# SwiGLU input projections of a decoder trunk: standing weights and 256 moving columns, from the third channel block on

## The chip, the cores and the metric

The kernel runs on one core of one Trainium2 chip. The metric is device time in microseconds (us), median of three runs; lower is better. The engines are named as in the profile: PE is TensorE, PEld its weight loads, DVE is VectorE, ACT is ScalarE, POOL is GpSimd, SP issues most DMAs. Of a matrix product one operand stands in the PE array (it is loaded by a weight load, LDWEIGHTS), the other one moves through it (MATMUL).

## The reference, cut to what matters

The trunk has 256 tokens of 1024 channels, two layers, and in each layer a SwiGLU, a token mixer and a second SwiGLU. There are thus four SwiGLU stages (f00, f01, f10, f11), and the change lies in them alone:

```
D_MODEL = 1024; SEQ = 256; D_FF = 2816

def swiglu(x, w_in, w_out):
    gate, up = jnp.split(x @ w_in, 2, axis=-1)
    return (jax.nn.silu(gate) * up) @ w_out

x = layer_norm(DN_ALPHA * x + 0.5 * swiglu(x, ffn_w_in[i, 0], ffn_w_out[i, 0]), ln_g[i, 0], ln_b[i, 0])
```

Everything is float32.

## The kernel before, in words

Products in float32 are made of three one-pass products of rounded values (type float32r). Each operand is split exactly into a rounded part and the rest: ACT casts (L113 for weights, L207 for activations), DVE subtracts (L114, L208). `mm3` (L199) then multiplies rounded by rounded (L201), rounded by weight rest (L202) and activation rest by rounded weight (L203), all into one accumulator in PSUM.

The 256 tokens are two blocks m of 128, the 2816 hidden channels are 11 blocks c of 256 (NB = 11). For a channel block c the input projection takes 256 gate columns and the 256 up columns that belong to them: 512 columns, in four weight units of 2 x 128 rows by 512 columns (`def_cols`). Before, the activations stand: `proj` loads 128 input channels by 128 tokens as weights (`lhsT=xs`) and moves 512 weight columns, so the PSUM bank holds 128 tokens by 512 columns (256 of gate, 256 of up). For a block c that is 2 token blocks x 8 groups of input channels x 3 = 48 products of 512 columns. `done` (L361 to L367) evacuates each bank: ACT takes Silu of the gate half (L365), DVE multiplies it by the up half (L366). The result `h` is tokens first, and the output projection needs it channels first, so `T(c)` (L369 to L380) turns it with four PE transposes of 128x128 (L376) into a PSUM bank `tp`, from where `split` (L206 to L208) makes `hT`. The output projection `O(c, m)` (L382) has `hT` standing and 512 columns of `ffn_w_out` moving: 12 products for each token block, into four accumulators (`acc`) that stay open over the whole stage.

The order on PE and SP is that of the list of operations: PE and SP are scheduled by hand, one operation after the other as `op` recorded them. In a stage the blocks c = 0 and 1 go first, one token block at a time (`proj_seq`, with T(0)); then for c = 2 to 10 the loop does the input projection of c for both token blocks (`proj_both`: four quarters), `T(c - 1)`, and the output products `O(c - 2, 0)` and `O(c - 2, 1)`. The stage ends with `O(8, 0)`, `T(10)`, `O(9, 0)`, `O(10, 0)`, the layer norm of token block 0, and `O(8..10, 1)`. Weight units come by DMA into four staging places and are split into a ring of ten (`Stream.advance`, called ahead of every operation). `mmp` has two PSUM banks for `mm`, `tp` two, `accp` four. `to_cm` (L218) makes the channels-first activations `xh` and `xl`, one pair of tiles for each token block.

Of the kernel before, what the change touches and what calls it, by code (L numbers as in the profile page):

```python
# [22 lines left out]
P = 128  # L23
# [29 lines left out]


class Stream:
    """Weight units in the order of their use: each is loaded ahead of time and split
    exactly into a rounded part and the rest, which one-pass products carry."""

    def __init__(self, tc, raw, wh, wl):
        self.tc, self.nc, self.raw, self.wh, self.wl = tc, tc.nc, raw, wh, wl  # L60
# [7 lines left out]
        return len(self.units) - 1  # L68

    def free(self, now, v):  # L70
        """The next place of the ring for unit v, if the work issued up to op `now` is done with it."""
        shut = min((i for i in self.shut if i > now), default=1 << 30)
        n = N_W + (N_WX if self.ext and self.last[v] < shut else 0)
        for d in range(n):
            t = (self.turn + d) % n
            u = self.ring[t]
            if u is None or self.last[u] <= now:
                return t
        return None

    def load(self, now, upto=None):
        """Load what the staging places allow after the work issued up to op `now`."""
        while len(self.loaded) < (upto or len(self.units)):
            v = len(self.loaded)
            o = v - N_RAW
            if o >= 0 and (len(self.done) <= o or o in self.native and self.last[o] > now):
                break
            t = self.raw.tile([P, 1024], F32, tag="raw", name=f"raw{v}")
            for view, src in self.units[v]:
                self.nc.sync.dma_start(view(t), src)  # L90
            self.loaded.append(t)

    def advance(self, now, ahead, upto=None):
        """Split the units that have a place, some ahead of use; `upto` must have one."""
        nc = self.nc
        self.top = max(self.top, -1 if upto is None else upto)
        n = len(self.units)
        self.load(now)
        while len(self.done) < min(n, self.top + 1 + ahead, len(self.loaded)):
            u = len(self.done)  # L100
            raw = self.loaded[u]
            if u in self.native:
                self.done.append((raw, None))
                continue
            t = self.free(now, u)
            if t is None:
                break
            hp, lp = (self.ext, self.ext) if t >= N_W else (self.wh, self.wl)
            self.ring[t] = u
            self.turn = t + 1  # L110
            h = hp.tile([P, 1024], F32R, tag=f"wh{t}", name=f"wh{u}", bufs=1)
            l = lp.tile([P, 1024], F32R, tag=f"wl{t}", name=f"wl{u}", bufs=1)
            nc.scalar.copy(h, raw)  # L113
            nc.vector.tensor_tensor(l, raw, h.bitcast(F32), op=ALU.subtract)  # L114
            self.loaded[u] = None
            self.done.append((h, l))
            self.load(now)
        assert upto is None or upto < len(self.done), "no place for a weight unit"
# [2 lines left out]
        return self.done[i]  # L121


class Builder:
    def __init__(self, tc, aps, pools):
        self.tc, self.nc, self.a = tc, tc.nc, aps
# [10 lines left out]
        self.first = {}  # L137

    def extra(self, kind):
        """The room next to the lasting pools: more weight units, or more 4 KB tiles."""  # L140
        if self.ext:
            self.ext.close()
        self.ext = contextlib.ExitStack()
        pool = self.ext.enter_context(self.tc.tile_pool(name="ext" + kind, bufs=1, reuse_waits="tile"))
        self.ws.ext = pool if kind == "w" else None
        self.xpool = pool if kind == "s" else None

# [1 line left out]
    def op(self, fn, *keys):  # L149
        self.ops.append((fn, keys, self.ahead))  # L150

    def flush(self):
        """The last normalisation of the stage before, behind the first work of this one."""
        if self.late:
            self.op(self.late)
        self.late = None
# [59 lines left out]
            evac(q, ps)  # L216

    def to_cm(self, src):  # L218
        """[tokens, channels] -> rounded part and rest, [channel, block of channels, token]."""
        h, l = self.s4("xh", F32R), self.s4("xl", F32R)  # L220

        def evac(q, ps):
            s = slice(q * 512, q * 512 + 512)
            self.split(h[:, s], l[:, s], ps)

        self.transpose8(src, evac)
        return h, l
# [42 lines left out]
        return xn  # L270

    def proj(self, ps, m, xs, key, us):
        """ps[128 tokens, 512] += x[m] @ units us of key (two blocks of 128 rows each)."""
        for u in us:
            h, l = self.w((key, u))
            for k in range(2):
                kk = 2 * u + k
                s = slice(k * 512, k * 512 + 512)
                c = slice(kk * P, kk * P + P)
                if l is None:  # L280
                    i = self.nc.tensor.matmul(ps, lhsT=xs[:, c], rhs=h[:, s], start=kk == 0, stop=kk == 7)  # L281
                else:
                    i = self.mm3(ps, xs[0][:, c], xs[1][:, c], h[:, s], l[:, s], kk == 0, kk == 7)
                self.first.setdefault(key, i)

    def def_cols(self, key, src, cols):
        """Units of src[1024, columns]: 2 blocks of 128 rows by 512 columns each."""
        v = src.rearrange("(k p) f -> p k f", p=P)
        w = 512 // len(cols)
        for u in range(4):  # L290
            parts = []
            for i, c in enumerate(cols):
                parts.append((
                    lambda t, i=i, w=w: t.rearrange("p (k g f) -> p k g f", k=2, f=w)[:, :, i, :],
                    v[:, 2 * u:2 * u + 2, c:c + w]))
            self.defs[key, u] = parts
# [5 lines left out]
        self.defs[key] = [(lambda t: t, src)]  # L302

    def proj_both(self, key, xs, done, between=None):
        """Both token blocks, two units at a time; between[i]: ops before the i-th quarter."""
        st = {}

        def go(m, us):
            def f():
                if m not in st:  # L310
                    st[m] = self.mmb()
                self.proj(st[m], m, xs()[m], key, us)
                if us[-1] == 3:
                    done(m, st[m])
            return f

        for i, (us, m) in enumerate((([0, 1], 0), ([0, 1], 1), ([2, 3], 0), ([2, 3], 1))):
            for fn in (between or {}).get(i, ()):
                self.op(fn)
            self.op(go(m, us), *[(key, u) for u in us])  # L320
# [15 lines left out]
                self.op(fn)  # L336
            self.op(go([2 * i, 2 * i + 1]), (key, 2 * i), (key, 2 * i + 1))

# [1 line left out]
    def ffn(self, i, j, S, hooks=(), store=None):  # L340
        nc = self.nc
        win, wout = self.a["ffn_w_in"][i, j], self.a["ffn_w_out"][i, j]
# [7 lines left out]

        def cm(m):
            def f():
                st["xs"][m] = self.to_cm(S["x"][m])
            return f

        def start():
# [12 lines left out]
        def T(c):  # L369
            def f():  # L370
# [7 lines left out]
                self.split(t[:, 0:512], t[:, 512:1024], ps)  # L378
                st["hT"][c] = t
            return f  # L380

        def O(c, m, ns=(0, 1)):  # L382
            def f():
# [31 lines left out]
        for c in range(2, NB):  # L415
# [3 lines left out]
                self.op(hooks[c == NB - 3])  # L419
            if c >= NB - 2:  # L420
                self.ahead = 99
            self.proj_both((tag, "i", c), xs, done(c))
            self.op(T(c - 1))
            if c >= 2 and c < NB - 1:
                O(c - 2, 0)
                O(c - 2, 1)
        L = NB - 1
        O(L - 2, 0)
        self.op(T(L))
        O(L - 1, 0)  # L430
        O(L, 0)
        self.ahead = AHEAD
# [3 lines left out]
                O(c, 1, ns)  # L436
        self.late = ln(1)

# [1 line left out]
    def sgu(self, S):  # L440
        nc = self.nc
        a = self.a
# [176 lines left out]
            O(3, i, 1)  # L619
        self.late = ln(1)  # L620

# [1 line left out]
    def rwkv(self, S):  # L623
        """The loads and the preparation that may come before the stage, and the stage."""
        nc = self.nc
        a = {k[5:]: v for k, v in self.a.items() if k.startswith("rwkv_")}
        V, G, A = nc.vector, nc.gpsimd, nc.scalar
# [101 lines left out]
            return f  # L729

        def lora1(m):
            """The first products of both small nets, with a row of ones below for the second's bias."""
            def f():
                ps = self.tpb()
                for i, x in enumerate((st["xf"][m], st["xx"][m])):
# [30 lines left out]
            return f  # L766

        def decay_x(m):
            """What stood before each token: the row above, or 1 at the start of a chunk."""
            def f():  # L770
                Ep, Em, Ex = st["E"][m]
                for c in range(2):
# [3 lines left out]
            return f  # L776

        def decay_w(m):
            """A chunk's last row is the decay of the whole chunk."""
            def f():  # L780
                if m == 0:
                    st["wc"] = self.small("wc", [P, 4, 8])
# [126 lines left out]
            return f  # L909

        def cm_kb(m, i, q):
            """Chunk 0 has its keys before its b's, chunk 1 behind."""
            def f():
                if i == 1 and q == 0:
                    st["KBT", m] = [self.s4("KBT") for q in range(2)]
# [141 lines left out]
        col = lambda h: slice((h // 2) * 64, (h // 2) * 64 + 64)  # L1057

        class Chunk:
            """One chunk of 64 tokens; v's in the half of the partitions that is the chunk's, u's in the other."""  # L1060

            def __init__(c_, ch):
                c_.ch, c_.m, c_.c = ch, ch // 2, ch % 2
# [8 lines left out]
            def at(c_, h, z, rows):  # L1072
                o = (h // 2) * P + z * 64
                return st["A"][c_.ch][h % 2][rows, o:o + 64]
# [294 lines left out]
```

## Time and profile before

| | |
|---|---|
| device time, three runs | 1148.21, 1146.11, 1149.02 us; median 1148.21 |
| span of the profiled execution | 1146.8 us |
| median less span | 1.4 us |
| PE busy | 1103.2 us, 96% of the span, 5854 products |
| DVE, ACT, POOL busy | 698.1, 481.2, 42.3 us |
| DMA | 216.51 MB, mean 189 GB/s |

The profiled execution's own time is known by its span alone; it lies within the three runs. Busy shares are means over the span: PE was at 100% in the SwiGLU stages, less in the RWKV stage and at the start. The length of a PE row is the time from a product's start to its modelled end, and the rows overlap; what a product costs in a stream is the distance from its start to the start of the next one.

### The profile page before, as it was taken

The numbers are of one execution on the slowest core, as the hardware profiler recorded it, in microseconds if no ns is written. First come the engines' busy times: TensorE is split into PE (matmuls) and PEld (weight loads), VectorE is DVE, ScalarE is ACT, GpSimd is POOL, SyncE is SP. The second block draws the span as 40 slices with busy tenths as digits, with TensorE's granted clock in tenths as the row PEclk, the third lists the DMA queues.
The fourth block names the chain that finished last, engine by engine and source line by source line (L and its number), as shares of the span: only waits on it lengthen the run. The fifth ranks groups of instructions, "written<-read, shape, count | busy, mean of one in ns | idle before, by whom it ended". The sixth has DMA issues, their size and how long they took to land.

```text
span 1146.8 us, 15330 instructions
## 1 busy us (share of the span) xinstructions
PE 1103.2 (96%) x5854; PEld 878.3 (77%) x5854; DVE 698.1 (61%) x964; ACT 481.2 (42%) x632; POOL 42.3 (4%) x44
## 2 busy tenths in 40 slices
PE   7999999999999999999999999999989889999997
PEld 5788888778888888888788888775555768888885
DVE  5654556769658555457655453878655788555544
ACT  5544444455335444444444452462123145444430
POOL 0000000100000000000000000112100110000000
PEclk9999999999999999999999999999998999999999
DMA  8776565776644766655567563437876135766631
GB/s 277 244 236 187 182 196 168 233 254 201 215 147 151 243 204 199 187 184 154 189 218 224 184 199 125 165 93 251 269 203 222 60 123 190 245 201 196 184 111 37
DMA packets 153788, 216.51 MB, mean 189 GB/s; under 512 B 21197, under 2 KB 114829, under 8 KB 153714
## 3 DMA queue, kind: packets, MB, share of 16 engines
q1 hardware_dynamic: 152250, 210.80, 57.5%
q0 software_dynamic: 1024, 3.15, 1.0%
q10 hardware_dynamic: 440, 1.57, 0.5%
q8 instruction: 46, 0.75, 0.3%
q14 instruction: 28, 0.23, 0.1%
HBM read 209.46 MB, written 3.42 MB: 186 GB/s over the span
## 4 chain that ended last, share of the span: by engine, by line
PE 77%; DVE 8%; DMA 7%; issue 3%; ACT 2%; SPq 1%; POOL 1%; ACTq 0%; DVEq 0%; POOLq 0%
PE mm L201 14%; PE mm L203 14%; PE mm L202 14%; PE acc L201 8%; PE acc L203 8%; PE acc L202 8%; PE mm L281 3%; DMA raw<-ffn_w_in 3%; DVE wl L114 2%; PE tp L376 2%; ACT wh L113 1%; DMA raw<-sgu_w_in 1%; POOL rs L239 1%; SPq L90 1%; PE tp L215 1%
## 5 line engine op out<-in xcount | busy, mean ns | idle before, releaser
L114 DVE TENSOR_TENSOR wl<-raw,wh 128x1024 fp32r<-128x1024 f32 x328 | 396.2, 1221 | 272.7 <-ACT wh L113 264.7
L113 ACT CAST wh<-raw 128x1024 fp32r<-128x1024 f32 x328 | 340.4, 1051 | 347.7 <-PE acc L203 144.1
L201 PE MATMUL mm<-wh,xh 128*128 128x512 f32 x832 | 327.6, 394 | 8.3 <-DVE h L366 3.8
L202 PE MATMUL mm<-wl,xh 128*128 128x512 f32 x832 | 325.1, 391 | 1.2 <-DVE wl L114 1.2
L203 PE MATMUL mm<-wh,xl 128*128 128x512 f32 x832 | 325.1, 391 | 0.2 <-DVE xl L208 0.2
L201 PEld LDWEIGHTS mm<-wh,xh 128*128 128x128 f32 x832 | 156.6, 188 | 44.9 <-DVE h L366 5.5
L202 PEld LDWEIGHTS mm<-wl,xh 128*128 128x128 f32 x832 | 156.6, 188 | 34.8 <-DVE wl L114 3.2
L203 PEld LDWEIGHTS mm<-wh,xl 128*128 128x128 f32 x832 | 156.5, 188 | 34.4 <-DVE xl L208 1.9
L201 PE MATMUL acc<-wh,hT 128*128 128x512 f32 x352 | 140.9, 400 | 0.0
L203 PE MATMUL acc<-wh,hT 128*128 128x512 f32 x352 | 137.6, 391 | 0.0
L202 PE MATMUL acc<-wl,hT 128*128 128x512 f32 x352 | 137.2, 390 | 0.0
L365 ACT ACTIVATE h<-mm 128x256 f32<-128x256 f32 x88 | 33.8, 384 | 104.1 <-PE mm L203 104.1
L203 PEld LDWEIGHTS acc<-wh,hT 128*128 128x128 f32 x352 | 66.1, 188 | 14.3
L202 PEld LDWEIGHTS acc<-wl,hT 128*128 128x128 f32 x352 | 66.3, 188 | 12.8
L201 PEld LDWEIGHTS acc<-wh,hT 128*128 128x128 f32 x352 | 66.1, 188 | 12.5
L366 DVE TENSOR_TENSOR h<-h,mm 128x256 f32<-128x256 f32 x88 | 36.7, 417 | 58.8 <-ACT h L365 58.8
L281 PE MATMUL mm<-raw,mix 128*128 128x512 f32 x128 | 60.6, 619 | 0.7 <-DMA raw<-rwkv_w_rkv 0.7
L239 POOL TENSOR_TENSOR rs<-ve,mhalf 128x1 f32<-128x1 f32 x14 | 14.1, 1010 | 928.0 <-DVE ve L247 928.0
L281 PEld LDWEIGHTS mm<-raw,mix 128*128 128x128 f32 x128 | 24.0, 196 | 27.2 <-issue 25.1
L208 DVE TENSOR_TENSOR hT<-tp,hT 128x512 fp32r<-128x512 f32 x44 | 30.1, 684 | 7.6 <-ACT hT L207 7.6
L207 ACT CAST hT<-tp 128x512 fp32r<-128x512 f32 x44 | 25.8, 587 | 9.0 <-PE tp L376 8.9
L261 DVE SCALAR_TENSOR_TENSOR y<-acc,x 128x512 f32<-128x512 f32 x24 | 15.9, 685 | 18.7 <-PE acc L203 18.7
(189 smaller groups left out, 878.4 us busy)
## 6 DMA issues: line engine op xcount, KB each, us to landing
raw<-ffn_w_in SPq DMA_DIRECT2D x352, 256.0 KB, 3.9
raw<-ffn_w_out SPq DMA_DIRECT2D x88, 512.0 KB, 3.9
raw<-rwkv_w_rkv SPq DMA_DIRECT2D x40, 512.0 KB, 4.0
raw<-sgu_w_in SPq DMA_DIRECT2D x32, 512.0 KB, 4.9
raw<-sgu_w_out SPq DMA_DIRECT2D x16, 512.0 KB, 3.5
raw<-rwkv_w_o SPq DMA_DIRECT2D x8, 512.0 KB, 3.5
lng<-ln_g SPq DMA_DIRECT2D x6, 512.0 KB
lnb<-ln_b SPq DMA_DIRECT2D x6, 512.0 KB
```

Of the source, the lines that this page charges most:

```text
L113: nc.scalar.copy(h, raw)
L114: nc.vector.tensor_tensor(l, raw, h.bitcast(F32), op=ALU.subtract)
L201: i = mm(out, lhsT=lh, rhs=rh, start=start, stop=False)
L202: mm(out, lhsT=lh, rhs=rl, start=False, stop=False)
L203: mm(out, lhsT=ll, rhs=rh, start=False, stop=stop)
L207: self.nc.scalar.copy(h, src)
L208: self.nc.vector.tensor_tensor(l, src, h.bitcast(F32), op=ALU.subtract)
L239: self.nc.gpsimd.tensor_tensor(rs, v, self.mhalf[:, :w], op=ALU.pow)
L281: i = self.nc.tensor.matmul(ps, lhsT=xs[:, c], rhs=h[:, s], start=kk == 0, stop=kk == 7)
L365: nc.scalar.activation(hb[:, o + 256:o + 512], ps[:, 0:256], AF.Silu)
L366: nc.vector.tensor_tensor(hb[:, o:o + 256], hb[:, o + 256:o + 512], ps[:, 256:512], op=ALU.mult)
L376: nc.tensor.transpose(ps[:, o:o + P], st["h"][c][:, hh:hh + P], self.ident)
```

## The change

From the third channel block (c = 2) to the last (c = 10) of each SwiGLU stage the roles in the input projection are exchanged. The weight unit stands: 128 input channels by 128 hidden channels of `h` or `l` are loaded into the array, and the activations of both token blocks move, 256 columns at a time. A product then gives 128 hidden channels by 256 tokens. A PSUM bank holds the gate of 128 hidden channels in its first 256 columns and the up of the same channels in the other 256; a block c has two such banks, j = 0 and 1. Silu and the multiplication have the same shape as before, but their result is already channels first, so `split` reads it from `hb` in SBUF, and the transposes `T(c)` remain for c = 0 and 1 only. For the moving operand the activations of both token blocks lie side by side: `Pair` holds two tiles of rounded parts and two of rests, each with four groups of input channels by 256 tokens, and the evacuation of the activations' transposes writes them in strips of 128. Blocks 0 and 1 still use `proj`, with the standing operand taken from `Pair.block`.

```
+class Pair:
+    def __init__(self, b):
+        self.b = b
+        self.h = [b.s4("xh", F32R) for q in range(2)]
+        self.l = [b.s4("xl", F32R) for q in range(2)]
+
+    def fill(self, src, m):
+        def evac(q, ps):
+            at = lambda t: t.rearrange("p (k m t) -> p k m t", k=4, m=2)[:, :, m, :]
+            self.b.split(at(self.h[q]), at(self.l[q]), ps.rearrange("p (k t) -> p k t", k=4))
+
+        self.b.transpose8(src, evac)
...
+    def both(self, k):
+        o = (k % 4) * 256
+        return self.h[k // 4][:, o:o + 256], self.l[k // 4][:, o:o + 256]
...
         def cm(m):
             def f():
-                st["xs"][m] = self.to_cm(S["x"][m])
+                if m == 0:
+                    st["X"] = Pair(self)
+                st["X"].fill(S["x"][m], m)
+                st["xs"][m] = st["X"].block(m)
             return f
...
+        def I(c):
+            key, ps = (tag, "i", c), []
+
+            def go(us):
+                def f():
+                    if us[0] == 0:
+                        ps[:] = [self.mmb(), self.mmb()]
+                        st["h"][c] = self.s4("h")
+                    ws = [self.w((key, u)) for u in us]
+                    mm = nc.tensor.matmul
+                    for j in range(2):
+                        for u, (h, l) in zip(us, ws):
+                            for k in range(2):
+                                xh, xl = st["X"].both(2 * u + k)
+                                for g in range(2):
+                                    out = ps[j][:, g * 256:g * 256 + 256]
+                                    o = k * 512 + g * 256 + j * P
+                                    first, last = u + k + g == 0, u == 3 and k == 1 and g == 1
+                                    mm(out, lhsT=h[:, o:o + P], rhs=xh, start=first, stop=False, skip_group_check=True)
+                                    mm(out, lhsT=l[:, o:o + P], rhs=xh, start=False, stop=False, skip_group_check=True)
+                                    mm(out, lhsT=h[:, o:o + P], rhs=xl, start=False, stop=last, skip_group_check=True)
+                        if us[-1] == 3:
+                            hb, b = st["h"][c], ps[j]
+                            s, s2 = slice(j * 256, j * 256 + 256), slice(512 + j * 256, 768 + j * 256)
+                            nc.scalar.activation(hb[:, s2], b[:, 0:256], AF.Silu)
+                            nc.vector.tensor_tensor(hb[:, s], hb[:, s2], b[:, 256:512], op=ALU.mult)
+                            if j == 1:
+                                t = st["hT"][c] = self.s4("hT", F32R)
+                                self.split(t[:, 0:512], t[:, 512:1024], hb[:, 0:512])
+                return f
+
+            for i in range(2):
+                us = [2 * i, 2 * i + 1]
+                self.op(go(us), *[(key, u) for u in us])
...
-            self.proj_both((tag, "i", c), xs, done(c))
-            self.op(T(c - 1))
+            I(c)
+            if c == 2:
+                self.op(T(1))
             if c >= 2 and c < NB - 1:
                 O(c - 2, 0)
                 O(c - 2, 1)
         L = NB - 1
         O(L - 2, 0)
-        self.op(T(L))
         O(L - 1, 0)
```

On PE, at the end of the input projection of c = 4 in the first SwiGLU stage, these rows stood before; a row names what is written, then the moving operand and the standing one, and the columns that move (`x4` is a run of four):

```order
L201 MATMUL mm<-wh_578,xh_248 128x512
L202 MATMUL mm<-wl_579,xh_248 128x512
L203 MATMUL mm<-wh_578,xl_249 128x512
L376 MATMUL tp<-ident,h_546 128x128 x4
L201 MATMUL acc<-wh_613,hT_568 128x512
```

And these stand there now:

```order
L434 MATMUL mm<-xh_124,wh_672 128x256
L435 MATMUL mm<-xh_124,wl_673 128x256
L436 MATMUL mm<-xl_126,wh_672 128x256
L229 MATMUL acc<-wh_707,hT_484 128x512
L230 MATMUL acc<-wl_708,hT_484 128x512
```

The four transposes are gone, operands have changed places, and the products have half the columns; a block has 96 of them where it had 48. The output products that follow are the same.

On ACT, in the evacuation of a middle block of that stage (`h` is Silu's result, `hT` the rounded part for the output products, `wh` a weight unit's rounded part), before:

```order
L365 ACTIVATE h_546<-mm 128x256
L113 CAST wh_653<-raw_575 128x1024
L365 ACTIVATE h_546<-mm 128x256
L113 CAST wh_659<-raw_582 128x1024
L207 CAST hT_568<-tp 128x512
```

Now:

```order
L440 ACTIVATE h_549<-mm 128x256
L113 CAST wh_772<-raw_669 128x1024
L440 ACTIVATE h_549<-mm 128x256
L113 CAST wh_778<-raw_676 128x1024
L235 CAST hT_662<-h_549 128x512
```

The places in the queue are the same; the cast of `hT` reads `h` of its own block from SBUF instead of a PSUM bank with the transposes of the block before it. DVE's order changes in the same way, and the DMA issues of SP stand as they stood.

## Rows read from the trace of the kernel before

**Rows 1.** The page: engines, PE's busy tenths and granted clock, the chain.
```profile
PE 1103.2 (96%) x5854; PEld 878.3 (77%) x5854; DVE 698.1 (61%) x964; ACT 481.2 (42%) x632; POOL 42.3 (4%) x44
...
PE   7999999999999999999999999999989889999997
...
PEclk9999999999999999999999999999998999999999
...
PE 77%; DVE 8%; DMA 7%; issue 3%; ACT 2%; SPq 1%; POOL 1%; ACTq 0%; DVEq 0%; POOLq 0%
```

**Rows 2.** Waits, whole span: us in total, times, longest.
```profile
ACT wh L113 <- PE acc L203: 144.1, 48, 8.5
ACT wh L113 <- PE mm L203: 126.3, 107, 4.8
ACT h L365 <- PE mm L203: 104.1, 80, 12.3
```

**Rows 3.** Chain that ended last, 60 to 184 us: start, duration, what.
```profile
65.56 0.44 PE tp L376 x4
...
99.16 0.44 PE tp L376 x4
...
183.17 0.44 PE tp L376 x4
```

**Rows 4.** PE's timeline in one block: start us, us, product.
```profile
115.80 0.60 PE L376 MATMUL tp<-ident,h 128*128 128x128 f32 x4
...
116.46 0.40 PE L202 MATMUL acc<-wl,hT 128*128 128x512 f32 x1
...
117.17 0.39 PE L202 MATMUL acc<-wl,hT 128*128 128x512 f32 x1
...
121.72 0.39 PE L201 MATMUL mm<-wh,xh 128*128 128x512 f32 x1
...
132.38 0.39 PE L203 MATMUL mm<-wh,xl 128*128 128x512 f32 x1
```

**Rows 5.** Windows: us, busy by engine (instructions), PEclk, DMA share, GB/s.
```profile
752.80:755.20 2.40, 2.40 (x7) 1.91 (x6) 1.52 (x3) 1.79 (x5) 0.00 (x0) 0.50 0.03 7
...
80.00:180.00 100.00, 100.00 (x454) 82.77 (x453) 51.60 (x54) 43.84 (x54) 0.00 (x0) 1.00 0.61 187
```

**Rows 6.** PE's timeline in the first of those windows.
```profile
753.15 0.63 PE L203 MATMUL mm<-wh,ml 128*128 128x512 f32 x1
...
755.28 0.63 PE L202 MATMUL mm<-wl,mh 128*128 128x512 f32 x1
```

**Rows 7.** Weight loads on the timeline: L738 (128 full-precision columns), and behind transposes.
```profile
729.18 1.86 PEld L738 LDWEIGHTS tp<-xf,w1a 128*128 128x128 f32 x16 [0.48 <-ACT xf L699]
730.96 0.53 PEld L738 LDWEIGHTS tp<-xx,w1a1m 128*128 128x128 f32 x4
...
116.12 0.19 PEld L201 LDWEIGHTS acc<-wh,hT 128*128 128x128 f32 x1
116.23 0.19 PEld L202 LDWEIGHTS acc<-wl,hT 128*128 128x128 f32 x1
```

**Rows 8.** Costliest groups by form: busy us, mean ns, idle before.
```profile
L201 PE MATMUL mm<-wh,xh 128*128 128x512 f32 x832 | 327.6, 394 | 8.3 <-DVE h L366 3.8 <-ACT wh L113 2.1 <-DVE vz L486 1.4
...
L202 PEld LDWEIGHTS mm<-wl,xh 128*128 128x128 f32 x832 | 156.6, 188 | 34.8 <-DVE wl L114 3.2
```

**Rows 9.** The page's costliest groups, on ACT and DVE.
```profile
L114 DVE TENSOR_TENSOR wl<-raw,wh 128x1024 fp32r<-128x1024 f32 x328 | 396.2, 1221 | 272.7 <-ACT wh L113 264.7
L113 ACT CAST wh<-raw 128x1024 fp32r<-128x1024 f32 x328 | 340.4, 1051 | 347.7 <-PE acc L203 144.1
...
L365 ACT ACTIVATE h<-mm 128x256 f32<-128x256 f32 x88 | 33.8, 384 | 104.1 <-PE mm L203 104.1
...
L366 DVE TENSOR_TENSOR h<-h,mm 128x256 f32<-128x256 f32 x88 | 36.7, 417 | 58.8 <-ACT h L365 58.8
...
L208 DVE TENSOR_TENSOR hT<-tp,hT 128x512 fp32r<-128x512 f32 x44 | 30.1, 684 | 7.6 <-ACT hT L207 7.6
L207 ACT CAST hT<-tp 128x512 fp32r<-128x512 f32 x44 | 25.8, 587 | 9.0 <-PE tp L376 8.9
```

More of the change, by code (lines that the diff above doesn't have):

```diff
@@ L121, in get, with block, at @@
         return self.done[i]
+class Pair:
[8 more added lines that the diff above has]
+        self.b.transpose8(src, evac)
+    def block(self, m):
+        def at(k):
+            o = (k % 4) * 256 + m * P
+            return self.h[k // 4][:, o:o + P], self.l[k // 4][:, o:o + P]
+        return at
+    def both(self, k):
+        o = (k % 4) * 256
+        return self.h[k // 4][:, o:o + 256], self.l[k // 4][:, o:o + 256]
 class Builder:
@@ L282, in proj @@
                 else:
-                    i = self.mm3(ps, xs[0][:, c], xs[1][:, c], h[:, s], l[:, s], kk == 0, kk == 7)
+                    xh, xl = xs(kk) if callable(xs) else (xs[0][:, c], xs[1][:, c])
+                    i = self.mm3(ps, xh, xl, h[:, s], l[:, s], kk == 0, kk == 7)
                 self.first.setdefault(key, i)
```

## The prediction

> **What bounds the kernel now.** I read the page's head first: PE is busy 96% of the span, its tenths are nines nearly everywhere, the granted clock stays at its upper level for most of the span, and 77% of the chain that ended last is PE [rows 1]. The reader is to see that one engine carries the time. Next the waits, to learn who waits for whom: ACT waits for PE in long sums, in casts of weights for a ring place and in Silu for a finished bank [rows 2]; work and slack on ACT and DVE lie behind PE, not ahead of it. Then the stage itself: from 80 to 180 us, inside the first SwiGLU stage, PE is busy 100.00 of 100.00 us at clock 1.00, while DVE has 51.60 and ACT 43.84 [rows 5]. There the time is the sum of the distances between starts on PE, and I price the change by these distances, since the busy lengths of PE rows overlap.
>
> The chain of this stage shows the four transposes of `T` once in every block: 65.56, 99.16 (two blocks on) and 183.17 us (seven blocks on) [rows 3]. So a block of the loop takes (183.17 - 65.56) / 7 = **16.80 us**. It holds 48 input products, 24 output products and four transposes. The input products of one block start at 121.72 (first) and 132.38 (last of 48) [rows 4]: 10.66 / 47 = **226.8 ns** each. The transposes stand in the chain with 0.44 us [rows 3], and three products behind them have a little more than that distance, 0.71 us from 116.46 to 117.17 [rows 4] where 3 x 226.8 makes 0.68.
>
> **What changes, part by part.** The changed loop runs nine times in each of four stages: 36 blocks.
>
> Removed: `T`, 36 times, with 0.44 us and the 0.03 us behind it.
>
> Exchanged: 48 products of 512 columns (48 x 0.2268 = 10.89 us) become 96 of 256 columns. What stays of a block is 16.80 - 10.89 - 0.44 - 0.03 = **5.44 us**, which is just its 24 output products at 226.8 ns. With p as the distance between two products of 256 columns, a block will take 5.44 + 96 p us, and the span changes by 36 x (5.44 + 96 p - 16.80). It is even at p = 11.36 / 96 = **118.3 ns**. Everything hangs on p, and no row shows this product: all rows of this type move 512 columns.
>
> What the rows do say of p. At the clock of 1.00, that is 2.4 GHz, 512 columns pass in 213.3 ns; the measured distance is 226.8, so 13.4 ns are over. In the window from 752.80 to 755.20 us the granted clock is 0.50, 1.2 GHz, [rows 5], and the same product goes from 753.15 to 755.28 in five steps [rows 6]: 426 ns, where 512 columns at 1.2 GHz take 426.7. There nothing is over. So the 13.4 ns are not cycles of the array that would double at the lower clock; something beside the array, of its own speed, needs 226.8 ns for such a product and is hidden when the array is slow. Two readings are open. Either it needs a fixed piece of time for each product, and then p = 106.7 + 13.4 = **120.1 ns**; or it hands over the columns at its own rate, and then p = 226.8 / 2 = **113.4 ns**.
>
> The second bound is the weight load, which a product of 256 columns has half the time to hide. Weight loads are long in their rows: 188 ns on the mean [rows 8]. But rows of loads overlap: at L738, sixteen pairs of load and product lie between 729.18 and 730.96 [rows 7], 111 ns a pair, and behind the transposes the load of the first output product starts at 116.12 and the next at 116.23 [rows 7], so the array was free for another after 110 ns. Thus p is at least 111 ns and a load fits into either reading. From above: if loads of this type could not overlap at all, p would be their 188 ns.
>
> I take 120.1. The nearest row is the same product, type and clock, and the half of it that is sure is the half that its columns explain; for a constant part per product speaks that each one has a step of its own, its load being put in place, whereas the other reading needs a supply that is just 6% slower than the array. That is a choice, about two to one, not a finding.
>
> The sum: 5.44 + 96 x 0.1201 = 16.97 us a block, 0.17 more than 16.80; x 36 = **+6.1 us**. Against the profiled execution that is 1146.8 + 6.1 = 1152.9 us of span. The median of the runs lies 1.4 us above that span, so the predicted time is **1154 us**, 0.5% more.
>
> A rule of the Trainium skill puts this otherwise. The page "TensorE: Matmul & The Clock Gate", section "Back-to-back issue gap", gives the distance at the upper clock as columns / 2.4 plus 2.5 ns; by it 256 columns cost 109.2 ns, the sum would be 36 x (5.44 + 10.48 - 16.80) = -31.7 us, and the time about 1117. The trace does not agree for this type: at 512 columns the rule says 215.8 and the rows 226.8.
>
> At nothing I cost the following. The evacuation keeps its shapes and its places in the queues: Silu 384 ns and the multiplication 417 ns, twice a block, one cast and one subtraction of 512 columns, 587 and 684 ns from PSUM [rows 9], now from SBUF; half of a weight unit's 1051 and 1221 ns [rows 9] is the price from there, 0.53 and 0.61 us. The cover is PE's next work: `hT` of a block is first used one block later, and in the tail of a stage behind `O(8, 0)` and `O(9, 0)`, 24 x 226.8 ns = 5.44 us. The chain from the last Silu to the last subtraction is 0.38 + 0.42 + 0.53 + 0.61 = 1.9 us, plus a weight cast and subtraction queued ahead (1.05 + 1.22), 4.2 us in all. With that cover gone it would cost what is left of 4.2 us, four times. The banks: j = 0 is evacuated a quarter of a block before the end, and 5.44 us of output products lie before the next block writes. Weight units are asked for two at a time as before, and are used up at the same rate; the split behind a freed place stays behind the same half block. The strips of 128 in `Pair.fill` are four casts and four subtractions a stage of the same 512 columns; only the start of a stage sees them, and I leave at most 1 us in all. DMA is unchanged.
>
> **The rivals.**
> *The columns' own rate* (other side): p = 113.4 to 116 ns, if the 13.4 ns halve with the columns and a load at 111 ns still fits. Then a block takes 16.33 to 16.58 us, the span changes by -17 to -8 us, and the time is 1131 to 1140. For it speaks that the excess vanishes altogether at the lower clock, as a supply rate would make it. It decides from p below 118.3. Chance 0.24, most of it near 1134.
> *In between*: p between 117.3 and 119.3 moves the span by less than 3.4 us either way. Chance 0.15, partly the lower edge of my forecast's reading.
> *Load and extra add up*: if the load's 111 ns and the 13.4 ns lie one behind the other, p = 124.7, a block 17.41 us, +22 us, 1170. For it speaks that half the cover is gone, against it that behind the transposes a load took only 110 ns with all it needed. Chance 0.12.
> *Loads that do not overlap*: p = 188 ns, a block 23.5 us, +241 us, 1389. Against it stand the 111 ns pairs [rows 7], though not of this type. Beside this: the Trainium skill, "Trainium Kernel Development and Optimization", section "Best Practices", would have distance to the limit judged by the busy share of weight loads. By that measure the change adds 48 loads to a block that has 76, and the loads' lengths would exceed the block; the trace speaks against it, since the lengths overlap. Chance 0.03.
> *The smaller constant*: if only about 2.5 ns of the excess stayed per product, p = 109 to 111, -29 to -25 us, 1119 to 1123; by the rows it would need loads at the very edge of what they show. The rule of the Trainium skill from "TensorE: Matmul & The Clock Gate", "Back-to-back issue gap", would lead here. Chance 0.03.
>
> **How the numbers follow.** About 0.3%, 3.4 us, is what a measurement of this kernel can tell from no change. My forecast, p = 119.3 to 123, has 0.43. With the two dearer rivals "slower" is 0.43 + 0.12 + 0.03 = 0.58; "same" 0.15; "faster" 0.24 + 0.03 = 0.27. The range: the cheaper side is cut at p = 113.4 (1132, rounded), the dearer at p = 123.5, where a block takes 17.30 us and the time is 1166; outside are the loads that do not overlap, the smaller constant, most of load and extra, and a little beneath 1132, some 0.2. The forecast's own range is 1150 to 1164.
>
> **What the changed profile would show.** The distance between starts of 128x256 products: 120 ns would bear me out, 113 the first rival, 125 or more the third; the count is 3456 such products and 32 transposes of `T`, in place of 1728 and 176. A block should have a period near 17.0 us, with PE still at 100% in the stages and no new idle time at the start of a block or ahead of `O(10, 0)`. If PE shows gaps ended by ACT or DVE there, my costing of the evacuation at nothing is wrong; a period that is longer than 5.44 us plus 96 distances says the same. The granted clock in the stages should stay at 1.00; if it falls, every distance here is void.

## The result, and the profile after

The changed kernel takes **1154.33 us** (median of four runs, 1152.46 to 1159.62); the kernel before, in the same comparison, 1147.16 us. The ratio is 1.0069, with a 95% interval of 1.0048 to 1.0089: 5.5 to 10.2 us slower. Forecast were 1154 us and +6.1 us; the two medians differ by 7.2 us.

The profiled execution of the changed kernel is the slowest of its four runs, so its span of 1157.5 us is not compared as a whole; distances between starts are. The page's head and its costliest groups, in the columns of [rows 1] and [rows 9]:

```profile
PE 1112.1 (96%) x7438; PEld 956.8 (83%) x7438; DVE 697.9 (60%) x964; ACT 483.3 (42%) x632; POOL 42.1 (4%) x44
...
PE 78%; DVE 8%; DMA 6%; issue 3%; ACT 3%; POOL 1%; ACTq 1%; SPq 0%; DVEq 0%; POOLq 0%
...
L434 PE MATMUL mm<-xh,wh 128*128 128x256 f32 x1152 | 327.4, 284 | 2.8 <-DVE h L398 2.8
L435 PE MATMUL mm<-xh,wl 128*128 128x256 f32 x1152 | 326.6, 284 | 0.0
L436 PE MATMUL mm<-xl,wh 128*128 128x256 f32 x1152 | 326.6, 284 | 0.0
...
L440 ACT ACTIVATE h<-mm 128x256 f32<-128x256 f32 x72 | 27.6, 384 | 101.0 <-PE mm L436 101.0
L441 DVE TENSOR_TENSOR h<-h,mm 128x256 f32<-128x256 f32 x72 | 30.1, 419 | 59.0 <-ACT h L440 59.0
```

There are 3 x 1152 = 3456 products of 256 columns, as counted, and little idle time ahead of them: 2.8 us in all 36 blocks, 2.0 of it at one place in the first stage. DVE and ACT are as busy as before. PE's timeline through one block, answering to [rows 4] (start us, us):

```profile
102.39 0.40 PE L229 MATMUL acc<-wh,hT 128*128 128x512 f32 x1
...
107.63 0.39 PE L231 MATMUL acc<-wh,hT 128*128 128x512 f32 x1
107.86 0.28 PE L434 MATMUL mm<-xh,wh 128*128 128x256 f32 x1
...
119.25 0.28 PE L436 MATMUL mm<-xl,wh 128*128 128x256 f32 x1
119.37 0.40 PE L229 MATMUL acc<-wh,hT 128*128 128x512 f32 x1
```

The block's 96 products start between 107.86 and 119.25: 11.39 / 95 = **119.9 ns** each. The period of the block is 119.37 - 102.39 = **16.98 us** (forecast 16.97; before 16.80).

### The profile page after: what moved, and what is told of

It is laid out like the page before. It is cut to its first block, busy times and chain, and to the rows that moved or that the text cites. A ratio compares the mean times of both kernels' runs of the same rounds, so it can differ in the third digit from the quotient of the medians.

```text
span 1157.5 us, 18493 instructions
## 1 busy us (share of the span) xinstructions
PE 1112.1 (96%) x7438; PEld 956.8 (83%) x7438; DVE 697.9 (60%) x964; ACT 483.3 (42%) x632; POOL 42.1 (4%) x44
## 4 chain that ended last, share of the span: by engine, by line
PE 78%; DVE 8%; DMA 6%; issue 3%; ACT 3%; POOL 1%; ACTq 1%; SPq 0%; DVEq 0%; POOLq 0%
PE mm L434 12%; PE mm L436 12%; PE mm L435 12%; PE acc L229 8%; PE acc L230 8%; PE acc L231 8%; PE mm L309 3%; PE mm L229 3%; PE mm L231 3%; PE mm L230 3%; DMA raw<-ffn_w_in 3%; DVE wl L114 2%; ACT wh L113 1%; DMA raw<-rwkv_w_rkv 1%; PE tp L243 1%
## 5 line engine op out<-in xcount | busy, mean ns | idle before, releaser
L434 PE MATMUL mm<-xh,wh 128*128 128x256 f32 x1152 | 327.4, 284 | 2.8 <-DVE h L398 2.8
L435 PE MATMUL mm<-xh,wl 128*128 128x256 f32 x1152 | 326.6, 284 | 0.0
L436 PE MATMUL mm<-xl,wh 128*128 128x256 f32 x1152 | 326.6, 284 | 0.0
L434 PEld LDWEIGHTS mm<-xh,wh 128*128 128x128 f32 x1152 | 221.6, 192 | 4.7 <-DVE h L398 3.4
L435 PEld LDWEIGHTS mm<-xh,wl 128*128 128x128 f32 x1152 | 221.8, 193 | 1.2
L436 PEld LDWEIGHTS mm<-xl,wh 128*128 128x128 f32 x1152 | 221.7, 192 | 0.0
L229 PE MATMUL mm<-wh,xh 128*128 128x512 f32 x256 | 102.6, 401 | 4.6 <-ACT wh L113 2.2
L230 PE MATMUL mm<-wl,xh 128*128 128x512 f32 x256 | 101.1, 395 | 0.6 <-DVE wl L114 0.5
L231 PE MATMUL mm<-wh,xl 128*128 128x512 f32 x256 | 100.9, 394 | 0.2 <-DVE xl L236 0.2
L229 PEld LDWEIGHTS mm<-wh,xh 128*128 128x128 f32 x256 | 48.6, 190 | 16.4 <-ACT wh L113 2.6
```

The source lines that it names most:

```text
L229: i = mm(out, lhsT=lh, rhs=rh, start=start, stop=False)
L230: mm(out, lhsT=lh, rhs=rl, start=False, stop=False)
L231: mm(out, lhsT=ll, rhs=rh, start=False, stop=stop)
L434: mm(out, lhsT=h[:, o:o + P], rhs=xh, start=first, stop=False, skip_group_check=True)
L435: mm(out, lhsT=l[:, o:o + P], rhs=xh, start=False, stop=False, skip_group_check=True)
L436: mm(out, lhsT=h[:, o:o + P], rhs=xl, start=False, stop=last, skip_group_check=True)
```

## The experiments

Each kernel ran with the kernel before beside it; ratios are to that one.

### The dropped transposes put back

```
             if c == 2:
                 self.op(T(1))
+            else:
+                self.op(U(c - 1))
...
         O(L - 2, 0)
+        self.op(U(L))
         O(L - 1, 0)
```

`U` is `T` without the split; nobody reads its bank.

> The changed kernel with the 36 dropped groups of four transposes put back on TensorE at their old places (their result is read by nobody). Theory (each row on TensorE's list costs its own distance, nothing hides it): 0.44 to 0.48 us a group, 36 groups, 16 to 17 us more than the changed kernel, about 1171 us, 2.0 to 2.3% above the kernel before. Rival (the transposes were hidden, and the change gained nothing by dropping them): no more than 2 us above the changed kernel, about 1155.

Measured: 1169.27 us, ratio 1.0198 (1.0177 to 1.0220). The chain that ended last shows the groups, start and us:

```profile
102.40 0.44 PE tp L421 x4
119.83 0.44 PE tp L421 x4
137.25 0.44 PE tp L421 x4
```

The period is 17.42 us, 0.44 more than the changed kernel's 16.98; the medians differ by 14.9 us, where 36 x 0.44 = 15.8 and 16 to 17 was expected. What the change removes is thus worth its distance on PE, and no more. The few slow products behind the transposes, for which I had added 0.03, did not show.

### The halves alone, with the old roles

```
+                elif key[0][0] == "f" and key[2] >= 2:
+                    mm = self.nc.tensor.matmul
+                    for g in range(2):
+                        out, s = ps[:, g * 256:g * 256 + 256], slice(k * 512 + g * 256, k * 512 + g * 256 + 256)
+                        a, z = kk + g == 0, kk == 7 and g == 1
+                        i = mm(out, lhsT=xs[0][:, c], rhs=h[:, s], start=a, stop=False, skip_group_check=True)
+                        mm(out, lhsT=xs[0][:, c], rhs=l[:, s], start=False, stop=False, skip_group_check=True)
+                        mm(out, lhsT=xs[1][:, c], rhs=h[:, s], start=False, stop=z, skip_group_check=True)
```

> The kernel before with its roles kept (activations stand, weights move) and its transposes kept, but each input product of 512 columns from the third channel block on cut into two of 256. Theory (a constant 13.4 ns for each product whatever stands in the array): 240 ns in place of 227 for each of 1728 products, 23 us more than before, about 1170 us, 1.9 to 2.1% above. Rival (the half product is dear because of the exchange: weights stand, and the standing operand comes from the split rather than from the activations): the halves run at 113 ns and the time is within 3 us of before.

Measured: 1165.98 us, ratio 1.0172 (1.0146 to 1.0198). On PE's timeline:

```profile
110.40 0.28 PE L288 MATMUL mm<-wl,xh 128*128 128x256 f32 x1
...
111.96 0.28 PE L289 MATMUL mm<-wh,xl 128*128 128x256 f32 x1
```

Thirteen steps in 1.56 us, 120 ns, with the activations standing as before. The block's period is 17.43 us, 0.63 more than before (from the starts of its output products). The price belongs to the product of 256 columns and not to the exchange of roles. The time is a little under the 1170 expected, which lies just above the interval (1163.1 to 1169.1 us on the 1146.38 of the kernel before); the lower end of the expected 1.9 to 2.1% lies in it.

### 128 columns

```
+                                    for b in range(2):
+                                        out = ps[j][:, g * 256 + b * P:g * 256 + b * P + P]
+                                        s = slice(b * P, b * P + P)
...
+                                        mm(out, lhsT=h[:, o:o + P], rhs=xh[:, s], start=first, stop=False, skip_group_check=True)
```

> The changed kernel with each product of 256 moving columns cut into two of 128, so 192 products a block. Theory (constant of 13.4 ns a product, and below that a floor by the weight load, which the rows of full-precision pairs put at 111 ns): the floor binds, 111 to 116 ns a product, a block 26.8 to 27.7 us, about 1500 to 1540 us, 31 to 34% above before. Rival (constant alone, loads never bind): 66.7 ns a product, a block 18.2 us, about 1200 us, 4 to 5% above. Rival (loads do not overlap, 188 ns): above 2000 us.

Measured: 1507.21 us, ratio 1.3154 (1.3132 to 1.3177). The second product of a block and the last one:

```profile
90.32 0.28 PE L437 MATMUL mm<-xh,wl 128*128 128x128 f32 x1
...
111.54 0.28 PE L438 MATMUL mm<-xl,wh 128*128 128x128 f32 x1
```

190 steps in 21.22 us: 111.7 ns; the block has 26.94 us, in the range expected. By the constant it would have been 66.7. That the weight load sets this pace I read from the order of the starts, here and in the changed kernel:

```profile
100.04 0.28 PE L437 MATMUL mm<-xh,wl 128*128 128x128 f32 x1
100.09 0.19 PEld L438 LDWEIGHTS mm<-xl,wh 128*128 128x128 f32 x1
100.15 0.28 PE L438 MATMUL mm<-xl,wh 128*128 128x128 f32 x1
```

```profile
108.21 0.28 PE L434 MATMUL mm<-xh,wh 128*128 128x256 f32 x1
108.21 0.19 PEld L435 LDWEIGHTS mm<-xh,wl 128*128 128x128 f32 x1
108.33 0.28 PE L435 MATMUL mm<-xh,wl 128*128 128x256 f32 x1
```

In the changed kernel the next load starts 2 to 3 ns behind a product's start, and its product 117 ns after that. With 128 columns the load starts 51 ns behind the product's start and its product only 60 ns after it, so the products now follow the loads, and loads follow each other every 111.7 ns. At 256 columns, 120 ns, they did not yet bind, but only 8 ns were left.

The agreement with the 111 ns pairs of [rows 7] is no support for this, though. Those are full-precision products, and a full-precision product of 512 columns takes 430 ns (eight of L281, 128 loads for 128 products, the last row 0.59 us long: (3.60 - 0.59) / 7), so 128 of its columns account for 107 of the 111 ns:

```profile
774.82 3.60 PE L281 MATMUL mm<-raw,mix 128*128 128x512 f32 x8
```

There, too, the load starts 2 ns behind the product before it. The pairs of [rows 7] were paced by their products; that the floor by the load has nearly the same number is luck. The loads behind transposes (116.12 and 116.23, [rows 7]) are the rows that showed it, 110 ns.

### The same standing operand twice in a row

```
                                     mm(out, lhsT=h[:, o:o + P], rhs=xh, start=first, stop=False, skip_group_check=True)
+                                    mm(out, lhsT=h[:, o:o + P], rhs=xl, start=False, stop=False, skip_group_check=True)
-                                    mm(out, lhsT=l[:, o:o + P], rhs=xh, start=False, stop=False, skip_group_check=True)
-                                    mm(out, lhsT=h[:, o:o + P], rhs=xl, start=False, stop=last, skip_group_check=True)
+                                    mm(out, lhsT=l[:, o:o + P], rhs=xh, start=False, stop=last, skip_group_check=True)
```

> The changed kernel with the order within three products changed: rounded weights by rounded activations, then the same rounded weights by the activations' rest, then the weight rest. Two products in a row thus name the same standing operand. Theory (the constant belongs to each product, its weight load is made again): 120 ns a product as before, a block of 16.98 us, 1152 to 1158 us. Rival (the constant is paid for a change of the standing operand): a third of the products at 109 ns, a block 0.35 us shorter, about 1142 us.

One run: 1156.58 us.

```profile
109.83 0.28 PE L434 MATMUL mm<-xh,wh 128*128 128x256 f32 x1
...
111.27 0.28 PE L434 MATMUL mm<-xh,wh 128*128 128x256 f32 x1
```

Twelve steps in 1.44 us, 120 ns. The constant is paid by every product, whether or not the product before it named the same standing operand. But naming it again did not spare the load: PE and PEld both have 7438 rows, as in the changed kernel. So the run does not part a constant of the product from one of putting its load in place.

### Two products in one

```
-                                    mm(out, lhsT=h[:, o:o + P], rhs=xh, start=first, stop=False, skip_group_check=True)
-                                    mm(out, lhsT=l[:, o:o + P], rhs=xh, start=False, stop=False, skip_group_check=True)
-                                    mm(out, lhsT=h[:, o:o + P], rhs=xl, start=False, stop=last, skip_group_check=True)
+                                    mm(out, lhsT=h[:, o:o + P], rhs=xhl, start=u + k == 0, stop=False, skip_group_check=True)
+                                    mm(out[:, 0:256], lhsT=l[:, o:o + P], rhs=xh, start=False, stop=u == 3 and k == 1, skip_group_check=True)
...
+                                nc.scalar.copy(tg, ps[j, g][:, 256:512])
+                                nc.vector.tensor_tensor(tg, tg, ps[j, g][:, 0:256], op=ALU.add)
```

> The changed kernel, but the rounded weights multiply the rounded activations and their rest in one product of 512 columns (the two lie side by side), into a bank of 512 columns; the weight rest's product of 256 columns adds to its first half, and ACT and DVE add the halves at the evacuation (two copies and two additions of 256 columns more for each j). Four banks a block, two of them from the transposes' pool. Theory (constant a product): a third of the block's input products falls away, 32 x 13.4 ns = 0.43 us a block, 15 us less than the changed kernel, about 1139, 0.6 to 0.9% below the kernel before. Rival (the longer evacuation holds banks and TensorE waits for it): 0.4 us or more of new waits a block, no better than the changed kernel, 1154 or above.

Measured: 1165.45 us, ratio 1.0163 (1.0144 to 1.0182): a miss, and the time lies on the rival's side, though the rival's mechanism holds only in part. Beside the lines above, `T(1)` stands behind `O(0, 0)` and `O(0, 1)` here, since the third block fills both `tp` banks. PE at the end of a block:

```profile
101.73 0.40 PE L433 MATMUL tp<-xhl,wh 128*128 128x512 f32 x1
...
103.14 0.40 PE L433 MATMUL tp<-xhl,wh 128*128 128x512 f32 x1
...
103.48 0.40 PE L228 MATMUL acc<-wh,hT 128*128 128x512 f32 x1
...
120.28 0.40 PE L228 MATMUL acc<-wh,hT 128*128 128x512 f32 x1
```

A pair takes 1.41 / 4 = 352 ns where 227 + 120 make 347, so the period is 16.80 us instead of 16.54: better than the changed kernel's 16.98, but 0.26 of the expected 0.44 us are gone, 0.16 of them in the 32 pairs. The rest was lost at the starts of the stages. In the third block of every stage PE waited for DVE (3.8, 2.6, 2.9 and 2.5 us in f00, f01, f10 and f11; the changed kernel 2.0, 0.4, none and 0.5), because both banks of j = 0 are needed at once and one of them had just been filled; after each of these four waits the granted clock was 0.50 for 3.4 us. And the first `T` came 3.2 us (f01) and 1.4 us (f10) later than in the changed kernel, counted from the layer norm ahead. The waits in f00 and f01, and two windows at the start of f01:

```profile
40.27 0.49 PE L433 MATMUL mm<-xhl,wh 128*128 128x512 f32 x1 [3.79 <-DVE h L397]
...
383.05 0.74 PE L433 MATMUL mm<-xhl,wh 128*128 128x512 f32 x1 [2.60 <-DVE h L397]
```

```profile
360.00:380.00 20.00, 18.99 (x89) 15.38 (x90) 14.38 (x23) 8.76 (x13) 0.92 (x1) 1.00 0.39 122
380.00:395.00 15.00, 12.40 (x62) 10.53 (x62) 7.77 (x10) 6.51 (x10) 0.00 (x0) 0.89 0.62 202
```

### The same, grouped, with the third block in the changed kernel's form

```
                                 for g in range(2):
                                     out = ps[j, g]
                                     o = k * 512 + g * 256 + j * P
                                     mm(out, lhsT=h[:, o:o + P], rhs=xhl, start=u + k == 0, stop=False, skip_group_check=True)
+                        for u, (h, l) in zip(us, ws):
+                            for k in range(2):
+                                xh, xhl = st["X"].both(2 * u + k)
+                                for g in range(2):
+                                    out = ps[j, g]
+                                    o = k * 512 + g * 256 + j * P
-                                    mm(out[:, 0:256], lhsT=l[:, o:o + P], rhs=xh, start=False, stop=u == 3 and k == 1, skip_group_check=True)
+                                    mm(out[:, 0:256], lhsT=l[:, o:o + P], rhs=xh, start=False, stop=u == 3 and k == 1, skip_group_check=True)
...
+            (I2 if c == 2 else I)(c)
```

> As two_for_one, with two things mended that its trace showed: within a quarter the eight products of 512 columns go first and the eight of 256 behind them (there they alternated, and a pair took 352 ns in place of 347), and the third channel block keeps the form of the changed kernel, so that TensorE does not wait for two banks at once at the start of a stage. Theory (the constant a product, and a switch of the column count costs a few ns): a block of 16.55 to 16.6 us in the middle of a stage, 32 blocks x 0.4 us less than in the changed kernel, 13 us, less what the finer cut of the activations still costs at the start of a stage (about 3 us each): 1150 to 1156 us. Rival (the pair is dear for another reason, such as writing two banks in turn): blocks stay at 16.8 us and the time is 1160 or above.

Measured: **1146.30 us**, ratio **0.9978 (0.9958 to 0.9999)**, ten runs; the kernel before had 1149.96 beside it. That is below the 1150 to 1156 expected. It is the lowest ratio here, but no clear gain: the difference is under the 0.3% that the prediction took as the least that can be told from no change, and beside other kernels the kernel before had medians of 1145.38 and 1146.38. `T(1)` is back at its place in the changed kernel. PE now, in runs of eight:

```profile
99.68 0.40 PE L232 MATMUL acc<-wh,hT 128*128 128x512 f32 x1
...
105.15 1.98 PE L474 MATMUL mm<-xhl,wh 128*128 128x512 f32 x8
106.97 1.11 PE L481 MATMUL mm<-xhl,wl 128*128 128x256 f32 x8
107.92 2.00 PE L474 MATMUL tp<-xhl,wh 128*128 128x512 f32 x8
...
110.71 2.00 PE L474 MATMUL mm<-xhl,wh 128*128 128x512 f32 x8
...
116.30 0.40 PE L232 MATMUL acc<-wh,hT 128*128 128x512 f32 x1
```

Eight of 512 and eight of 256 columns take 107.92 - 105.15 = 2.77 us; 8 x 0.347 = 2.78. The next sixteen, which follow products of 256 columns, take 2.79. So the 5 ns of a pair were the changes between column counts, of which a little is left, and the period is 16.62 us.

Against the kernel before, in the two traces: from the first `T` to the layer norm the four stages together are 8.4 us shorter, and the first `T` comes 9.0 us later in all (the activations are evacuated in quarters here; what that costs by itself was not run). The blocks gain what the starts lose. Against the changed kernel the starts cost 1.5 us a stage where about 3 were expected, and the longer wait and the low clock in f00 are gone; by the traces that is what put the time below the range.

### The activations' tiles alone

This is the kernel before with `Pair` in place of `to_cm` in the SwiGLU stages, and nothing else changed.

```
-                st["xs"][m] = self.to_cm(S["x"][m])
+                if m == 0:
+                    st["X"] = Pair(self)
+                st["X"].fill(S["x"][m], m)
+                st["xs"][m] = st["X"].block(m)
```

> The kernel before, with the changed kernel's tiles for the activations alone (two tiles of rounded parts and two of rests, filled in strips for each half of the channels); products, transposes and blocks are those of before. Theory (the tiles' two halves are no longer evacuated back to back at the start of f10 and f11, a weight split stands between them): blocks at 16.80 us, but the first transposes of T come about 31.5 us (f10) and 34.8 us (f11) after the layer norm ahead of them, where before had 30.9 and 32.6; the time 2 to 3 us above before. Rival (the changed kernel's later starts come from its products, or from weights that arrive later): 30.9 and 32.6 us again, and a time within 1 us of before.

Measured: 1147.55 us, ratio 1.0007 (0.9991 to 1.0024), twelve runs. By time alone this decides nothing. The trace decides the place: `T` starts 31.39 us (f10) and 34.11 us (f11) behind the first BN_AGGREGATE of the layer norm, against 30.85 and 32.60 in the kernel before and 31.62 and 34.76 in the changed one. On ACT, at the start of f10, the casts of the two halves:

```profile
536.79 0.58 ACT L235 CAST xh<-tp 128x512 fp32r<-128x512 f32 x1 [1.83 <-PE tp L243]
537.43 1.05 ACT L113 CAST wh<-raw 128x1024 fp32r<-128x1024 f32 x1
538.39 0.58 ACT L235 CAST xh<-tp 128x512 fp32r<-128x512 f32 x1
```

A weight's cast stands between them, as in the changed kernel (the last three rows below) and not in the kernel before (the first row):

```profile
538.78 1.07 ACT L207 CAST xh<-tp 128x512 fp32r<-128x512 f32 x2 [1.83 <-PE tp L215]
```

```profile
542.60 0.59 ACT L235 CAST xh<-tp 128x512 fp32r<-128x512 f32 x1 [1.79 <-PE tp L243]
543.44 1.05 ACT L113 CAST wh<-raw 128x1024 fp32r<-128x1024 f32 x1 [0.26 <-DMA raw<-ffn_w_in]
544.39 0.58 ACT L235 CAST xh<-tp 128x512 fp32r<-128x512 f32 x1
```

The kernel of halves with the old roles has the old tiles, and its starts are those of before, 30.90 and 32.55 us. So 2.0 us of the changed kernel's 2.9 us at these two starts come from the tiles; the other 0.9 us I have not separated. That this lengthens the whole time is not shown: the interval, -1.0 to 2.7 us, holds both nothing and the 2 us.

## Why the prediction was right

**The distance p.** "I take 120.1" was called a choice, two to one. It is measured: 119.9 ns in the changed kernel, 120 with the old roles. With 226.8 ns for 512 columns [rows 4] the two points lie on a line of 0.417 ns a column, which is 1 / 2.4 GHz, and a constant of 13.3 ns for each product. The rival of the columns' own rate, 113.4 ns, is out.

**The lower clock.** I had reasoned that the 13.4 ns are not cycles of the array, since nothing is over at 1.2 GHz [rows 5, 6]. The changed kernel has such a stretch too, in its first stage, where the granted clock is 0.50:

```profile
42.20 0.41 PE L434 MATMUL mm<-xh,wh 128*128 128x256 f32 x1
...
44.76 0.41 PE L434 MATMUL mm<-xh,wh 128*128 128x256 f32 x1
...
41.90:44.90 3.00, 3.00 (x16) 3.00 (x15) 1.97 (x2) 1.14 (x2) 0.00 (x0) 0.50 0.76 260
```

Twelve steps in 2.56 us, 213.3 ns: 256 columns at 1.2 GHz and nothing more. The constant is hidden there also at 256 columns.

**The weight load.** "At least 111 ns" is where the kernel with 128 columns landed. The rows it was first read from, the pairs at L738, do not show it, as said at the 128 columns; the loads behind transposes do. The third rival, load and extra one behind the other at 124.7 ns, and loads that do not overlap are out with it. The Trainium skill, "TensorE: Matmul & The Clock Gate", section "LDWEIGHTS (loading the stationary operand)", gives a load's time as columns / 1.2, 106.7 ns for 128; the 111.7 measured agrees to 5 ns.

**The sum.** A block was to grow by 0.17 us and grew by 0.18. The whole agrees less cleanly. In us, from the two traces, with a layer norm placed at its first BN_AGGREGATE:

| | f00 | f01 | f10 | f11 |
|---|---|---|---|---|
| first `T` of the stage to the next layer norm, before | 158.19 | 157.28 | 158.91 | 157.37 |
| the same, now | 161.79 | 158.73 | 158.52 | 158.79 |
| layer norm ahead (f00: the program's start) to the first `T`, before | 35.59 | 30.62 | 30.85 | 32.60 |
| the same, now | 35.34 | 30.75 | 31.62 | 34.76 |

The first two rows differ by 6.1 us in all, as forecast, but only f01 and f11 (1.4 us each) show what nine blocks grew by and nothing else. In f00 (+3.6) PE waited 0.6 us longer in the third block, and the granted clock, which stayed at 1.00 there before, fell behind that wait to 0.50 for 3.4 us: some 16 products took 213 instead of 120 ns, 1.5 us. In f10 (-0.4) a wait of 1.6 us that the kernel before had is gone. The products that waited, before and now:

```profile
40.29 0.50 PE L201 MATMUL mm<-wh,xh 128*128 128x512 f32 x1 [1.33 <-DVE h L366]
...
567.48 0.50 PE L201 MATMUL mm<-wh,xh 128*128 128x512 f32 x1 [1.64 <-DVE h L366]
```

```profile
40.78 0.39 PE L434 MATMUL mm<-xh,wh 128*128 128x256 f32 x1 [1.97 <-DVE h L398]
```

The sum had no term for any of these. That they nearly cancel is luck, and so is a median within 1 us of the forecast. Two of the signs that the prediction named for being wrong, new idle time at the start of a block and a granted clock below 1.00 in a stage, did appear, at this one place in f00.

**What I had under-sized.** Of the strips in `Pair.fill` I wrote "I leave at most 1 us in all". The starts of f10 and f11 are 0.8 and 2.2 us later, 2.9 us; the other two moved by less than 0.3. What that term had wrong is that only the shapes of these casts and subtractions were priced: the order on ACT moved, a weight's cast now stands between the halves, and that pushes back the activations' second half and the layer norm of the other token block behind it on DVE. With all four starts (2.8 us) the SwiGLU stages take 6.1 + 2.8 = 8.9 us more in the traces; the runs' interval of 5.5 to 10.2 holds both 6.1 and 8.9 and does not decide. The rest of the 10.7 us between the two profiled spans lies in stages that did not change.

**The evacuation at nothing** held in the blocks: the idle time ahead of the first products, 3.8 us for `h` in [rows 8], became 2.8 us. In the third block of f00 it did not quite hold, 2.0 us for 1.3.

**Slips in the working.** The smaller constant at 109 ns makes -32 us and 1116, not -29 and 1119; 113.4 ns makes 1131, not 1132; the lower edge of the forecast, 119.3 ns, makes 1152, not 1150. `hT` of a block is first used two blocks later, not one, so its cover was larger than said. None of them changes the forecast.

## What to carry to other kernels

Price a product by the distance between starts in rows of its own type, split into columns and a constant; a change that halves the columns pays the constant twice, here 13.3 ns x 1728 = 23 us against 16 us for the transposes it saved. Before weights are made to stand because of the output's orientation, count the moving columns: with 256 of them a block lost 0.18 us. Joining two products into one of 512 columns, issued in runs of eight of each length, made a block 0.18 us shorter than before, but the starts of the stages took that back (0.9978, not clear of no change). And keep the order on the in-order queues in view at a stage's start: a tile cut in two let another operation in between. Last, a sum that comes out right over the whole kernel can hide errors that cancel; compare it stage by stage.

## What was not expected of the hardware

- A change of column count on PE costs: alternating 512 and 256 columns, a pair took 352 ns; in runs of eight 346 to 349.
- PEld was busy 113.30 of 120 us in the changed kernel's blocks, which loads did not bind, and 77.01 of 80 us with 128 columns, where loads bind:

```profile
60.00:180.00 120.00, 120.00 (x852) 113.30 (x851) 60.34 (x63) 52.00 (x63) 0.00 (x0) 1.00 0.65 196
```

```profile
100.00:180.00 80.00, 80.00 (x643) 77.01 (x642) 25.70 (x27) 21.74 (x27) 0.00 (x0) 1.00 0.38 119
```

So a busy share of 94% for loads does not tell that they bind; the distance between products, against 111.7 ns, does, and so does the place of the load's start behind the product before it (2 to 3 ns or 51).
- What in the hardware the constant of 13.3 ns is, stays open. It does not go with the roles, nor with naming another standing operand, and is not seen at 1.2 GHz. Nor is it seen at full-precision products, each with its own load: 430 ns at L281 are 3 more than twice 213.3. Whether it belongs to the product or to putting its load in place, no run here parts.
